# A third pair of seven-product units in three of the four blocks of keys and values

## The chip, the cores and the metric

One NeuronCore of a Trainium2 chip runs the whole kernel. The metric is the device time of one execution in microseconds (us). The engines are named as in the profile: PE (TensorE, the products), PEld (its loading of the stationary operand), DVE (VectorE), ACT (ScalarE), POOL (GpSimd) and SP (SyncE, which issues the transfers).

## The reference

One layer of an encoder on 256 frames of width 2048 in float32: a half-step feed-forward (SwiGLU), a mixer, a cross-attention to 256 memory tokens, and a second half-step feed-forward. The change touches the cross-attention only, and there the projection of the memory to keys and values:

```python
def mem_cross_attention(h, mem_h, w_q, w_kv, w_o):
    b, s, _ = h.shape
    q = (h @ w_q).reshape(b, s, XATTN_HEADS, XATTN_HEAD_DIM)
    kv = (mem_h @ w_kv).reshape(b, mem_h.shape[1], 2, XATTN_HEADS, XATTN_HEAD_DIM)
    k, v = kv[:, :, 0], kv[:, :, 1]
    logits = jnp.einsum('bshd,bmhd->bhsm', q, k).astype(jnp.float32) * (XATTN_HEAD_DIM ** -0.5)
    p = jax.nn.softmax(logits, axis=-1).astype(v.dtype)
    o = jnp.einsum('bhsm,bmhd->bshd', p, v).reshape(b, s, D_MODEL)
    return o @ w_o
```

There are 4 heads of 512 columns; `w_kv` is 2048 x 4096, keys in the first half of the columns, values in the second.

## The kernel before

**Precision by parts.** Every float32 operand of a product is held as a high part (rounded to the type fp32r) and a low part (what the rounding left). A product of two such operands takes three matmuls: high by high, high by low, low by high (`products`, L357 to L362). In this text a *product* is one such matmul of 128 x 128 by 128 x 512.

**Units.** All weights pass through the kernel once, in units of 1 MB (128 x 2048 float32). A unit is loaded by SP into one of three `raw` tiles, split by ACT (high part `wh`, L1579) and DVE (low part `wl`, L453; near the end of a block POOL takes 768 of the 2048 columns), and used by PE. The class `Stream` writes all this out in order: splits run two units ahead of PE (`AHEAD`), the load of unit u + 3 is issued behind the split of unit u, and `st.op(f, n)` puts other work behind n further units. `wh` and `wl` have three buffers each. A scheduler then settles the order in each engine's queue by a timeline of its own.

**Blocks.** A block is eight units: all 2048 rows of a weight matrix, 256 rows a unit, by 1024 columns. A plain unit (`unit_p` in `block_s`) does 24 products. The cross-attention has blocks of queries, then, for each half of the heads, a block of keys and a block of values, then blocks of the output projection. In the loop over b near the end of the change's region, each block of keys is followed by the turning of the keys (`turn_K`), the logits and softmax of two heads (`logits`, then `probs`, which turns the probabilities with PE transposes at L1341), all placed among the first units of the block of values; the products of values with probabilities (`values`, L1358) fall among the first units of the block after.

**Seven products.** Some units are computed as a 2 x 2 product with seven multiplications in the place of eight (`seven`, L493 to L509, Strassen's scheme in Winograd's form): 21 products instead of 24. For this the unit's weights need sums (`split_seven`: DVE makes T in three operations at L486; ACT and DVE split T into `wh` and `wl`, 4 x 512 columns, and three of the four raw quarters into `xh` and `xl`, L279 and L280), and the pair of row groups of the activations needs sums too, made once for all blocks that use that pair (`Sums.make`, L424 to L437, kept in the tile `ye` and partly in `xs` itself). The results P1 to P7 go to two pairs of PSUM accumulators: P2, P4, P3 and P0 hold what plain units add to as well, P1, P6 and P7, P5 only serve the turned units. `combine` (L574 to L579) and `join` (L589) bring them together at the end of the block.

**PSUM.** One pool of four tiles serves accumulators, transposes, logits and the products with values alike. The pair for P1, P6, P7, P5 can thus only be opened when the softmax or `values` has given its tiles back.

**Homes.** In the cross-attention the tiles for T, `xh` and `xl` are not their own: `shared_tile` takes them in turn from a list of tags (`homes`). For keys and values, T lies in `sg` (two buffers of 2048 columns, which also hold the blocks' combined results) and `xh` and `xl` in `att` (two buffers of 1536 columns). So the raw parts of one unit fill both buffers of `att`. Keys and values themselves lie in `kv`, two buffers of 2048 columns.

**Order.** `kv_sums` names the pairs with sums, here 0 and 4. `KV_ORDER` is the order of the eight units in each block, so units 0 and 4 stand at the fourth and seventh places.

Of the kernel before, what the change touches and what calls it, by code (L numbers as in the profile page):

```python
# [15 lines left out]
D = 2048  # L16
# [4 lines left out]
NB = 512  # L21
# [78 lines left out]
def build(ctx, tc, I, out):  # L100
# [89 lines left out]
    xs = main.tile([P, KT, 2, S], F32R, tag="xs", name="xs")  # L190
# [79 lines left out]
    def among_weights(f):  # L270


        scalar, vector = behind_weights(f)
        latest["vector"] = vector
        if scalar is not None:
            latest["scalar"] = scalar
# [349 lines left out]
    def wload(dst, w, k0, n, n0, cols=NB):  # L626
        nc.sync.dma_start(
            dst, w[k0 * P : (k0 + n) * P, n0 : n0 + cols].rearrange("(k p) n -> p k n", p=P)
        )
# [9 lines left out]
    def wwide(w, n0, k0=0, nk=KT):  # L639

        def src(k):
            def load(raw):
                raw = raw.rearrange("p (k n) -> p k n", n=2 * NB)
                if len(loaded) < 3:
                    for kk in range(2):
                        parts = (0, NB) if not loaded else (0,)
                        for c in parts:
                            n = 2 * NB // len(parts)
                            wload(raw[:, kk : kk + 1, c : c + n], w, k + kk, 1, n0 + c, n)
                else:  # L650
                    wload(raw, w, k, 2, n0, 2 * NB)
                next(first_loads, None)
                loaded.append(1)
            return load
        return [src(k0 + k) for k in range(0, nk, 2)]
# [557 lines left out]
    for b in range(2):  # L1213
        block_b(wblock(w_in, (4 + b) * NB), xs, ev_v(b))
        for i in range(2):
# [12 lines left out]
                 "xl": [("att", 3 * NB, 2), ("PT", D, 1)]}  # L1228
    Q_HOMES = {"T": [("sg", D, 2)], "xh": [("att", 3 * NB, 2)],
               "xl": [("PT", D, 1), ("att", 3 * NB, 2)]}  # L1230
    KV_HOMES = {"T": [("sg", D, 2)], "xh": [("att", 3 * NB, 2)], "xl": [("att", 3 * NB, 2)]}

    def homes(of):
        return lambda: scope.update(shared={tag: list(of[tag]) for tag in of})
# [27 lines left out]
    def mem_fold(c):  # L1262

        v = four(ptile(uid("tm")))
        for j in range(4):
            for h in range(2):
                nc.tensor.transpose(  # L1267
                    v[:, j, h * P : (h + 1) * P],
                    xa[f"mem{h}"][:, c * NB + j * P : c * NB + (j + 1) * P], ident,
                )  # L1270
        split_four(xs, 4 * c, v, G_MEM)
# [10 lines left out]
    w_q, w_kv, w_o = I["xattn_w_q"][0], I["xattn_w_kv"][0], I["xattn_w_o"][0]  # L1282
# [2 lines left out]
    q_sums, Q_ORDER = Sums("ye", xs, (4, 5), True, 2), ((0, 1, 2, 3, 6, 4, 5, 7),  # L1285
                                                        (0, 1, 4, 2, 5, 3, 6, 7))
    Q_SEVENS = ((4,), (4, 5))
    kv_sums, KV_ORDER = Sums("ye", xs, (0, 4), True, 2), (1, 5, 2, 0, 3, 6, 4, 7)
    held = {}

    def ev_Q(b):
# [10 lines left out]
    def turn_K(h):  # L1302
        v = rows_turned(held["K", h])
        K = xa["K", h] = xt("K", [P, 4, 2, M], F32R, tag="kv", bufs=2)
        split(K[:, :, 0, :], K[:, :, 1, :], v)

    def ev_V(b):
        def evict(j, c):
            V = xa["V", 2 * b + j] = xt("V", [P, 2, 2, XHD], F32R, tag="kv", bufs=2)
            split(V[:, :, 0, :], V[:, :, 1, :], c)  # L1310
        return evict

    def logits(h):
        ps = ptile(uid("pl"))
        for t in range(2):
            tok = slice(t * P, (t + 1) * P)
            parts = [(d, a, b) for d in range(4) for a, b in ((0, 0), (0, 1), (1, 0))]
            for i, (d, a, b) in enumerate(parts):
                nc.tensor.matmul(  # L1319
                    ps[:, t, :M], ys[:, 4 * h + d, a, tok], xa["K", h][:, d, b, :],  # L1320
                    start=i == 0, stop=i == 11,
                )
        scale = XHD ** -0.5
        nm, sm = xt("nm", [P, 2], bufs=2), xt("sm", [P, 2], bufs=2)
        nc.vector.tensor_reduce(out=nm, in_=ps[:, :, :M], axis=AX.X, op=ALU.max)
        nc.vector.tensor_scalar_mul(nm, nm, -scale)
        pr = xa["P", h] = xt("P", [P, 2, M], bufs=2)
        for t in range(2):
            nc.scalar.activation(
                pr[:, t, :], ps[:, t, :M], AF.Exp, scale=scale, bias=nm[:, t : t + 1],  # L1330
                accum_out=sm[:, t : t + 1],
            )
        nc.vector.reciprocal(out=sm, in_=sm)
        for t in range(2):
            nc.vector.tensor_scalar_mul(pr[:, t, :], pr[:, t, :], sm[:, t : t + 1])

    def probs(h):
        ps = ptile(uid("pt"))
        for mtile in range(2):
            for t in range(2):  # L1340
                nc.tensor.transpose(  # L1341
                    ps[:, mtile, t * P : (t + 1) * P], xa["P", h][:, t, mtile * P : (mtile + 1) * P], ident
                )
        if h % 2 == 0:
            xt("PT", [P, D], F32R)
        PT = xa["PT", h] = xa["PT"][:, h % 2 * 4 * S : (h % 2 + 1) * 4 * S].rearrange(
            "p (m a s) -> p m a s", m=2, a=2
        )
        split(PT[:, :, 0, :], PT[:, :, 1, :], ps[:, :, :S])

    def values(h):
        for p in range(2):
            ps = ptile(uid("pv"))
            for d in range(2):
                col = slice((2 * p + d) * P, (2 * p + d + 1) * P)
                parts = [(m, a, b) for m in range(2) for a, b in ((0, 0), (0, 1), (1, 0))]
                for i, (m, a, b) in enumerate(parts):
                    nc.tensor.matmul(  # L1358
                        ps[:, d, :S], xa["V", h][:, m, a, col], xa["PT", h][:, m, b, :],
                        start=i == 0, stop=i == 5,  # L1360
                    )
            split_pair(ys, 4 * h + 2 * p, ps[:, :, :S])
# [3 lines left out]
    for b in range(2):  # L1366
# [3 lines left out]
        if b == 0:  # L1370
            for c, after in enumerate((5, 7, 6, 9)):
                st.op(lambda c=c: mem_fold(c), after)
    st.op(homes(KV_HOMES))
    for g, after in zip(kv_sums.pairs, (0, 2)):
        st.op(lambda g=g: among_weights(lambda: kv_sums.make(g)), after)
    for b in range(2):
        block_s(wwide(w_kv, b * 2 * NB), xs, kv_sums, KV_ORDER, lambda j, c, b=b: held.__setitem__(
            ("K", 2 * b + j), c))
        for j in (1, 0):
            h = 2 * b + j  # L1380
            st.op(lambda h=h: turn_K(h), 1)
        for h in (2 * b, 2 * b + 1):
            st.op(lambda h=h: logits(h), 2)
            st.op(lambda h=h: probs(h), 3)
        block_s(wwide(w_kv, D + b * 2 * NB), xs, kv_sums, KV_ORDER, ev_V(b))
        for h in (2 * b, 2 * b + 1):
            st.op(lambda h=h: values(h), 1)
# [211 lines left out]
def program(shapes):  # L1599
    import concourse.bacc as _bacc  # L1600

    nc = _bacc.Bacc("TRN2", target_bir_lowering=False, num_devices=1)
    args = {
        name: nc.dram_tensor(f"in_{name}", shapes[name], F32, kind="ExternalInput").ap()
        for name in _INS
    }
    out = nc.dram_tensor("out", _OUT, F32, kind="ExternalOutput").ap()
    with tile.TileContext(nc, schedule_with_timeline_sim=True) as tc, ExitStack() as ctx:
        build(ctx, tc, args, out)
    return nc  # L1610
# [10 lines left out]
```

## Time and profile before

| | |
|---|---|
| median of 3 runs | 2083.8 us (2082.58 to 2084.51) |
| the profiled execution: its own time | 2082.87 us |
| its span, first to last instruction | 2081.1 us |
| granted clock of PE, mean | 0.999 |

Rows of the timeline give the start in us, the length in us, the engine, line, operation, out<-in, and in brackets the idle time before it and what ended it. Rows of grouped views end with busy us, mean ns of one, idle us before. Rows of windows give the stretch, its length, then busy us (and count) of PE, PEld, DVE, ACT and POOL, then the granted clock, the share of the DMA engines, and GB/s. In the timeline a product's row lasts longer than the distance to the next one's start, since products overlap; the ends of products are modelled.

### The profile page before, as it was taken

The numbers are of one execution on the slowest core, as the hardware profiler recorded it, in microseconds if no ns is written. First come the engines' busy times: TensorE is split into PE (matmuls) and PEld (weight loads), VectorE is DVE, ScalarE is ACT, GpSimd is POOL, SyncE is SP. The second block draws the span as 40 slices with busy tenths as digits, with TensorE's granted clock in tenths as the row PEclk, the third lists the DMA queues.
The fourth block names the chain that finished last, engine by engine and source line by source line (L and its number), as shares of the span: only waits on it lengthen the run. The fifth ranks groups of instructions, "written<-read, shape, count | busy, mean of one in ns | idle before, by whom it ended". The sixth has DMA issues, their size and how long they took to land.

```text
span 2081.1 us, 24343 instructions
## 1 busy us (share of the span) xinstructions
PE 2069.6 (99%) x9660; PEld 1727.6 (83%) x9660; DVE 1786.6 (86%) x1670; ACT 1138.7 (55%) x1128; POOL 98.4 (5%) x87
## 2 busy tenths in 40 slices
PE   9999999999999999999999999999999999999998
PEld 7888888888888888888888888888888888888886
DVE  7998899989998677679788777879988999889987
ACT  7655455644654545455755444656554555545554
POOL 0000000000000000000000000000100010000001
PEclk9999999999999999999999999999999999999999
DMA  7666666566656755557655455666576665676664
GB/s 264 207 201 227 235 223 219 185 223 239 227 199 218 249 167 182 162 185 272 226 179 190 162 182 180 205 222 203 181 242 212 237 207 193 223 242 222 210 226 151
DMA packets 131178, 435.95 MB, mean 209 GB/s; under 512 B 9844, under 2 KB 13528, under 8 KB 130680
## 3 DMA queue, kind: packets, MB, share of 16 engines
q1 hardware_dynamic: 130888, 433.86, 61.9%
q8 instruction: 76, 1.25, 0.2%
q10 hardware_dynamic: 176, 0.53, 0.1%
q14 instruction: 38, 0.31, 0.0%
HBM read 417.58 MB, written 16.78 MB: 209 GB/s over the span
## 4 chain that ended last, share of the span: by engine, by line
PE 99%; DMA 0%; DVE 0%; ACT 0%; SPq 0%; DVEq 0%; issue 0%; ACTq 0%
PE pt L362 59%; PE pt L507 27%; PE pa L347 7%; PE pb L362 2%; PE ph L780 1%; PE pl L1319 1%; PE pv L1358 1%; PE px L791 1%; PE pp L1012 0%; PE pe L362 0%; DMA x<-in_x 0%; PE pa L1039 0%; PE po L1161 0%; PE tm L1267 0%; PE px L717 0%; PE pq L1148 0%
## 5 line engine op out<-in xcount | busy, mean ns | idle before, releaser
L362 PE MATMUL pt<-wh,xs 128*128 128x512 f32 x2128 | 682.4, 390 | 0.1
L453 DVE TENSOR_TENSOR wl<-raw,wh 128x2048 fp32r<-128x2048 f32 (+1 forms) x256 | 552.1, 2162 | 141.7 <-ACT wh L1579 141.3
L1579 ACT CAST wh<-raw 128x2048 fp32r<-128x2048 f32 x256 | 489.4, 1913 | 300.7 <-PE pt L362 134.5
L362 PEld LDWEIGHTS pt<-wh,xs 128*128 128x128 f32 x2128 | 398.7, 188 | 81.9 <-ACT xs L236 0.4
L362 PE MATMUL pt<-wh,ys 128*128 128x512 f32 x1472 | 463.9, 389 | 0.0
L489 ACT CAST wh<-T 128x1024 fp32r<-128x1024 f32 x236 | 248.1, 1055 | 366.7 <-DVE T L486 355.8
L362 PE MATMUL pt<-wl,xs 128*128 128x512 f32 x1064 | 414.5, 390 | 0.0
L362 PEld LDWEIGHTS pt<-wh,ys 128*128 128x128 f32 x1472 | 276.2, 188 | 56.9
L362 PE MATMUL pt<-wl,ys 128*128 128x512 f32 x736 | 286.8, 390 | 0.0
L453 DVE TENSOR_TENSOR wl<-T,wh 128x2048 fp32r<-128x2048 f32 (+1 forms) x118 | 264.7, 2243 | 0.8 <-ACT wh L489 0.4
L362 PEld LDWEIGHTS pt<-wl,xs 128*128 128x128 f32 x1064 | 199.8, 188 | 41.0
L280 DVE TENSOR_TENSOR xl<-raw,xh 128x1536 fp32r<-128x1536 f32 x118 | 206.7, 1751 | 18.9 <-ACT xh L279 18.9
L279 ACT CAST xh<-raw 128x1536 fp32r<-128x1536 f32 x118 | 174.6, 1480 | 44.0 <-PE pt L507 35.1
L486 DVE TENSOR_TENSOR T<-T,raw 128x512 f32<-128x512 f32 x236 | 162.9, 690 | 6.2
L362 PEld LDWEIGHTS pt<-wl,ys 128*128 128x128 f32 x736 | 138.2, 188 | 28.6
L486 DVE TENSOR_TENSOR T<-raw 128x1024 f32<-128x1024 f32 x118 | 143.8, 1218 | 0.5
L507 PE MATMUL pt<-wh,xs 128*128 128x512 f32 x364 | 141.8, 390 | 0.0
L457 POOL TENSOR_TENSOR wl<-raw,wh 128x768 fp32r<-128x768 f32 x40 | 74.1, 1852 | 1376.2 <-DVE wl L453 1339.2
L507 PE MATMUL pt<-xh,xs 128*128 128x512 f32 x364 | 135.8, 389 | 0.0
L347 PE MATMUL pa<-xs,wh 128*128 128x512 f32 x384 | 135.6, 397 | 0.0
L507 PE MATMUL pt<-wh,xe 128*128 128x512 f32 x320 | 124.3, 389 | 0.0
L347 PE MATMUL pa<-xs,wl 128*128 128x256 f32 x384 | 106.8, 282 | 0.0
(248 smaller groups left out, 2312.4 us busy)
## 6 DMA issues: line engine op xcount, KB each, us to landing
raw<-in_ffn_w_down SPq DMA_DIRECT2D x88, 1024.0 KB, 5.6
raw<-in_ffn_w_up SPq DMA_DIRECT2D x80, 1024.0 KB, 5.0
raw<-in_ffn_w_gate SPq DMA_DIRECT2D x77, 1024.0 KB, 5.1
raw<-in_w_in SPq DMA_DIRECT2D x32, 1024.0 KB, 5.3
raw<-in_xattn_w_kv SPq DMA_DIRECT2D x32, 1024.0 KB, 5.0
raw<-in_w_out SPq DMA_DIRECT2D x16, 1024.0 KB, 5.6
raw<-in_xattn_w_q SPq DMA_DIRECT2D x16, 1024.0 KB, 5.6
raw<-in_xattn_w_o SPq DMA_DIRECT2D x16, 1024.0 KB, 5.6
```

What stands on the lines that cost most here:

```text
L279: in_turn("scalar", lambda: nc.scalar.copy(hi, src))
L280: in_turn("vector", lambda: nc.vector.tensor_tensor(out=lo, in0=src, in1=f32(hi), op=ALU.subtract))
L347: nc.tensor.matmul(o, w, x, start=k == 0 and i == 0, stop=last and i == 1)
L362: nc.tensor.matmul(ps, a, w, start=first and i == 0, stop=last and i == 2)
L453: in_turn("vector", lambda: nc.vector.tensor_tensor(out=lo[:, :n], in0=src[:, :n], in1=f32(hi[:, :n]), op=ALU.subtract))
L457: rest = nc.gpsimd.tensor_tensor(out=lo[:, n:], in0=src[:, n:], in1=f32(hi[:, n:]), op=ALU.subtract)
L486: in_turn("vector", lambda: nc.vector.tensor_tensor(out=o, in0=a, in1=b, op=ALU.add))
L489: in_turn("scalar", lambda: nc.scalar.copy(th[:, c], t[:, c]))
L507: nc.tensor.matmul(banks[n], x, w, start=n in fresh and j == 0, stop=n in ends and j == 2)
L780: nc.tensor.transpose(v[:, i, h * P : (h + 1) * P], g[:, h, i * P : (i + 1) * P], ident)
L791: nc.tensor.transpose(v[:, j, h * P : (h + 1) * P], x[:, h, j * P : (j + 1) * P], ident)
L1579: in_turn("scalar", lambda: nc.scalar.copy(hi, raw))
```

## The change

A third pair, 2, joins the sums of keys and values, and its unit is computed with seven products in three of the four blocks: both blocks of values and the second block of keys. The first block of keys keeps its order and its two seven-product units, since there the sums of pair 2 are only being made. In the three other blocks the order changes so that the turned units stand at places 4 (pair 0), 6 (pair 4) and 7 (pair 2). The list of homes for `xh` and `xl` is written out by turns: the middle one of the three takes its raw parts to the tiles of keys and values (`kv`), the two others to `att` as before.

```diff
-    KV_HOMES = {"T": [("sg", D, 2)], "xh": [("att", 3 * NB, 2)], "xl": [("att", 3 * NB, 2)]}
+    KV_TURNS = [("att", 3 * NB, 2)] * 2 + [("att", 3 * NB, 2), ("kv", D, 2), ("att", 3 * NB, 2)] * 3
+    KV_HOMES = {"T": [("sg", D, 2)], "xh": KV_TURNS, "xl": KV_TURNS}
...
-    kv_sums, KV_ORDER = Sums("ye", xs, (0, 4), True, 2), (1, 5, 2, 0, 3, 6, 4, 7)
+    kv_sums = Sums("ye", xs, (0, 4, 2), True, 3)
+    KEY_ORDER, KV_ORDER = (1, 5, 2, 0, 3, 6, 4, 7), (1, 5, 3, 0, 6, 4, 2, 7)
...
-    for g, after in zip(kv_sums.pairs, (0, 2)):
+    for g, after in zip(kv_sums.pairs, (0, 2, 5)):
         st.op(lambda g=g: among_weights(lambda: kv_sums.make(g)), after)
     for b in range(2):
-        block_s(wwide(w_kv, b * 2 * NB), xs, kv_sums, KV_ORDER, lambda j, c, b=b: held.__setitem__(
-            ("K", 2 * b + j), c))
+        block_s(wwide(w_kv, b * 2 * NB), xs, kv_sums, KV_ORDER if b else KEY_ORDER,
+                lambda j, c, b=b: held.__setitem__(("K", 2 * b + j), c),
+                sevens=() if b else (0, 4))
```

## The prediction

> **What bounds the kernel now.** I read the page first (busy shares, the chain of waits), then the waits of PE, then the windows of the cross-attention, then its timeline.
>
> ```profile
> span 2081.1 us, 24343 instructions
> PE 2069.6 (99%) x9660; PEld 1727.6 (83%) x9660; DVE 1786.6 (86%) x1670; ACT 1138.7 (55%) x1128; POOL 98.4 (5%) x87
> PE 99%; DMA 0%; DVE 0%; ACT 0%; SPq 0%; DVEq 0%; issue 0%; ACTq 0%
> ```
>
> ```profile
> PE pwarm L206 <- POOL ident masks.py:199: 1.4, 1, 1.4
> PE px L717 <- DMA x<-in_x: 0.8, 1, 0.8
> ```
>
> The chain is PE from end to end, and the view of waits puts only two against it, both at the start. A product left out is therefore time saved, and a wait of PE is time added. Nothing later makes it good, as PE has no slack to give back.
>
> ```profile
> 1135.00:1186.00 51.00, 51.00 (x261) 43.36 (x261) 36.47 (x36) 25.00 (x27) 3.47 (x3) 1.00 0.49 165
> 1186.00:1234.00 48.00, 48.00 (x236) 40.68 (x235) 34.31 (x28) 22.91 (x20) 3.74 (x3) 1.00 0.53 175
> 1234.00:1284.00 50.00, 50.00 (x257) 42.57 (x256) 35.66 (x35) 23.38 (x25) 3.02 (x3) 1.00 0.51 167
> 300.00:420.00 120.00, 120.00 (x539) 99.55 (x538) 114.70 (x88) 71.03 (x59) 7.42 (x4) 1.00 0.61 201
> ```
>
> The first three windows are the three blocks that change (first values, second keys, second values); the fourth is a stretch of the first feed-forward. The columns after the times are busy us of PE, PEld, DVE, ACT, POOL. DVE is 72% busy in the three blocks and 96% in the feed-forward, whose PE is as dense. So on average DVE has room for more work here; what decides is the order inside a block.
>
> The one place late in the run where PE does wait is too short for the view of waits, but the timeline has it, in the block of queries:
>
> ```profile
> 1062.74 0.39 PE L507 MATMUL pt<-xl,xs 128*128 128x512 f32 x1
> 1062.97 0.39 PE L507 MATMUL pt<-xh,xs 128*128 128x512 f32 x1
> ...
> 1066.49 0.50 PE L507 MATMUL pt<-xl,xs 128*128 128x512 f32 x1
> 1066.83 0.39 PE L507 MATMUL pt<-xh,xs 128*128 128x512 f32 x1
> ...
> 1068.98 0.50 PE L507 MATMUL pt<-wl,xs 128*128 128x512 f32 x1
> ```
>
> ```profile
> 1063.17 1.48 ACT L279 CAST xh<-raw 128x1536 fp32r<-128x1536 f32 x1 [11.12 <-PE pt L507]
> 1064.55 1.99 ACT L489 CAST wh<-T 128x1024 fp32r<-128x1024 f32 x2
> ```
>
> ```profile
> 1064.68 1.76 DVE L280 TENSOR_TENSOR xl<-raw,xh 128x1536 fp32r<-128x1536 f32 x1 [4.33 <-ACT xh L279]
> 1066.63 2.29 DVE L453 TENSOR_TENSOR wl<-T,wh 128x2048 fp32r<-128x2048 f32 x1 [0.19 <-ACT wh L489]
> ```
>
> These rows give four prices. A product costs 0.227 us from start to start (1062.74 to 1062.97), though each row lasts 0.39. When PE has read the last of a 7-product unit's raw low part at time a, the next such unit's raw parts may be cast into the freed tile: ACT starts at a + 0.43, the new low raw part reaches PE at a + 3.75 (1066.49), the low part of the sums at a + 6.24 (1068.98). The first product after a wait comes 0.34 later instead of 0.227, so each wait costs 0.11 more than itself.
>
> **The change part by part.** *Products removed.* A plain unit has 24 products, a 7-product one 21. One more unit is turned in each of three blocks: 9 products by 0.227 = -2.04 us. That is all it can win, 0.10% of the time.
>
> *The third set of sums* adds seven VectorE and two ScalarE operations, once, in the first block of keys. The order of the built program puts them between the two splits that end and begin here:
>
> ```profile
> L424 DVE TENSOR_TENSOR j<-xs 128x512 f32<-128x512 f32 x1 | 0.7, 686 | 0.0
> L286 DVE TENSOR_TENSOR ye<-j,ye 128x384 fp32r<-128x384 f32 x1 | 0.6, 550 | 0.0
> L432 DVE TENSOR_TENSOR j<-j 128x128 f32<-128x128 f32 x1 | 0.3, 293 | 0.0
> ```
>
> ```profile
> 1121.67 2.29 DVE L453 TENSOR_TENSOR wl<-raw,wh 128x2048 fp32r<-128x2048 f32 x1
> 1126.80 1.49 DVE L453 TENSOR_TENSOR wl<-raw,wh 128x1280 fp32r<-128x1280 f32 x1 [2.85 <-ACT wh L1579]
> ```
>
> ```profile
> 1129.37 0.39 PE L362 MATMUL pt<-wh,xs 128*128 128x512 f32 x1
> ```
>
> Six of them, 0.69 + 5 x 0.29 = 2.1 us, go ahead of the first row, and 2.85 us stand idle behind it; the seventh (0.55) comes after the second row, where DVE waits again: nothing. The unit of the first row is then split by 1126.1, 3 us before PE begins it (third row); without the gap that would be the cover.
>
> *More split work.* Each turned unit adds three sums and a raw low part on DVE, 1.22 + 2 x 0.69 + 1.76 = 4.4 us, against about 14 us that DVE idles in each block:
>
> ```profile
> L1579 ACT CAST wh<-raw 128x2048 fp32r<-128x2048 f32 x7 | 13.4, 1913 | 10.5 <-PE pt L362 6.8 <-issue 3.4 <-ACT wh L1579 0.3
> L453 DVE TENSOR_TENSOR wl<-raw,wh 128x2048 fp32r<-128x2048 f32 x4 | 9.2, 2290 | 3.4 <-ACT wh L1579 3.4
> ...
> L280 DVE TENSOR_TENSOR xl<-raw,xh 128x1536 fp32r<-128x1536 f32 x2 | 3.5, 1756 | 4.2 <-ACT xh L279 4.2
> ...
> L486 DVE TENSOR_TENSOR T<-T,raw 128x512 f32<-128x512 f32 x4 | 2.8, 690 | 0.1
> L486 DVE TENSOR_TENSOR T<-raw 128x1024 f32<-128x1024 f32 x2 | 2.4, 1218 | 0.0
> ```
>
> Weight transfers keep their number and order; the loads behind places 6 and 7 start up to 2 us later and are wanted over 5 us after that. Cost nothing.
>
> *Middle unit's raw parts in the tiles of keys and values.* In a block of values the cast of the middle unit's high raw part now stands in ACT's queue ahead of the first softmax, and waits until PE has done the first head's logits:
>
> ```profile
> 1153.53 0.69 DVE L1325 TENSOR_REDUCE nm<-pl 128x2 f32<-128x512 f32 x1 [1.56 <-PE pl L1319]
> 1156.86 0.17 DVE L1333 RECIPROCAL sm<-sm 128x2 f32<-128x2 f32 x1 [2.43 <-ACT P L1329]
> 1157.06 0.62 DVE L1335 TENSOR_SCALAR P<-P,sm 128x256 f32<-128x256 f32 x2
> ```
>
> ```profile
> 1154.51 1.28 ACT L1329 ACT_TABLE_LOAD   x1 [4.86 <-DVE nm L1326]
> ```
>
> Logits end at 1153.5, the cast runs to 1155.0, so the table load starts 0.5 us late. Following both queues on with the durations above, the first head's probabilities are ready at 1158.8 and the second's at 1166.5.
>
> ```profile
> 1158.73 0.39 PE L507 MATMUL pt<-xh,xs 128*128 128x512 f32 x1
> ...
> 1160.55 0.60 PE L1341 MATMUL pt<-ident,P 128*128 128x128 f32 x4
> ...
> 1161.22 0.40 PE L362 MATMUL pt<-wh,xs 128*128 128x512 f32 x1
> ```
>
> PE begins place 4 at 1158.73; four transposes cost 1161.22 - 1160.55 - 0.227 = 0.44. In the new order PE turns the first probabilities after 13 products (1161.7, 2.9 us to spare) and the second after 20 + 9 more (1168.7, 2.2 us to spare). Nothing, by those margins. In the second block of keys they wait for the first values' last product; 27 products, 6.1 us, lie between that and their use, and the low part takes 1.76: nothing.
>
> *Places 6 and 7 side by side.* The raw parts of place 7 go into the tile of place 4. Both before and after, these are free late, as PE puts off the twelve of place 4's products that go into P1, P6, P7 and P5 until the softmax gives up its PSUM tiles. Before, a plain unit still lay between:
>
> ```profile
> 1169.67 0.39 PE L507 MATMUL pt<-xl,xs 128*128 128x512 f32 x1
> ...
> 1176.24 0.39 PE L507 MATMUL pt<-xl,xs 128*128 128x512 f32 x1
> ```
>
> ```profile
> 1170.09 1.48 ACT L279 CAST xh<-raw 128x1536 fp32r<-128x1536 f32 x1 [5.79 <-PE pt L507]
> ```
>
> From the last read to the next use 6.57 us passed, and 3.75 are needed. In the new order 13 products and three transposes lie between, 14 x 0.227 + 0.33 = 3.50. So in each block of values, counted from a:
> - wait 1, low raw part: ready 3.75, reached 3.50: 0.25.
> - wait 2, low part of the sums: eight products on PE reaches it at 3.75 + 0.34 + 7 x 0.227 = 5.68; ready 6.24: 0.56.
> - wait 3: all 18 products of P7 and P5 of the three units now come in a row, from 7.26 on, because their accumulator is only freed by the second head's probabilities. The sixth, at 8.39, is the last to read place 4's weights, and only then may ACT cast place 8: 8.39 + 0.43 + 1.91 + 0.04 + 2.29 + 0.06 = 13.12. PE does the other twelve and two of place 8 and stands before its low part at 11.79: 1.33.
>
> Sum 2.14, with 3 x 0.11 behind the waits 2.47, and 0.09 for transposes that now stand in three groups instead of two: 2.56 a block, 5.1 us for both. Behind the waiting product everything on PE stands; ACT and DVE only gain lead. The bounds of the unseen wait 3 are nothing (place 8 finds another buffer) and, if the cast had to wait for all 18, 4.0; I take 1.33, as the built program names the sixth. In the second block of keys no probabilities hold the accumulators: 29 products lie between place 4's last raw read and place 7's first, 6.8 us. No wait.
>
> *Sum.* -2.04 + 5.1 = +3.1 us. The profiled run took 2082.87 (span 2081.1 and 1.8 around it): 2086.0. The median of the runs is 0.93 above it: **2086.9**.
>
> **The rivals.**
> - *The waits don't come* and the nine products are won: 2083.8 - 2.0 = 2081.8. For it: 2.47 us a block rests on margins of 0.25 to 1.33, and DVE is 72% busy. Against: the queries' block shows two of the three waits at just these distances.
> - *The softmax takes over* (slower). ACT casts the middle unit's parts between the two exponentials, DVE sums between the two heads, and PE waits in order for the second head's transposes. It decides once the chain is more than the 2.2 us late. If a raw low part and a low part of sums (1.76 + 2.29) came ahead of the second probabilities, 1.85 us a block would be added: 2086.9 + 3.7 = 2090.6. Against: the built order has them behind.
> - *PE's clock falls in the waits* (slower). If the 24 products of place 8 ran at half rate after a wait, 5.4 us a block would be added: 2097.8. The granted clock is the column before the DMA share; it is 1.00 in the windows above and lower only where PE did nothing for microseconds, after its last product:
>
> ```profile
> 2076.00:2081.00 5.00, 0.00 (x0) 0.00 (x0) 0.49 (x2) 0.20 (x1) 0.00 (x0) 0.59 0.63 236
> ```
>
> The Trainium skill ("TensorE: Matmul & The Clock Gate", "HAM oscillation — how this bites in real kernels") puts the limit at PE gaps over about 3.4 us; by that rule waits of 1.33 leave the sum as it is, and no run here shows the limit itself.
>
> **How the numbers follow.** The forecast 0.60, no waits 0.20, softmax 0.16, clock 0.04. A measurement of this kernel can tell about 0.2%, 4.2 us, from no change. The forecast's own range is 2085.3 to 2088.5 (0.8 us a block either way); about an eighth of it lies beyond 2088.0. Slower by over 0.2%: 0.08 + 0.15 + 0.04 = 0.27. Faster by as much needs more than the nine products: 0.01. Within: 0.72. The range takes in the no-wait case and the softmax's up to its price, and leaves out the clock: 2081.3 to 2090.5.
>
> **What would show it.** In the profile after: nine L362 and L507 products fewer; three gaps between starts of products in each block of values, before a low raw part, a low part of sums from T, and the low part of the plain unit that ends the block, the last the longest; DVE at about 80% there; no gap before the transposes of P and none in the second block of keys. Wrong: no gaps (rival one), gaps before the transposes of P (rival two), products 0.4 us apart or a clock under 1 (rival three).

## The result, and the profile after

| | before | after |
|---|---|---|
| median | 2083.39 us (2082.58 to 2084.51) | 2086.61 us (2085.95 to 2089.36) |
| span of the profiled execution | 2081.1 us | 2084.1 us |

The ratio is 1.0016, with a 95% interval of 1.001 to 1.0022: slower by 3.2 us, where 3.1 were forecast (2086.9, reckoned from a median before of 2083.8). Below are the line of busy times after, and the windows of the three blocks that changed (first values, second keys, second values; the columns are those of the prediction). Each window ends at the product at which the window of before ends.

```profile
PE 2069.3 (99%) x9651; PEld 1724.8 (83%) x9651; DVE 1800.0 (86%) x1689; ACT 1143.4 (55%) x1136; POOL 98.6 (5%) x87
```

```profile
1135.05:1187.85 52.80, 51.30 (x258) 42.51 (x258) 38.90 (x39) 26.44 (x29) 2.42 (x3) 1.00 0.44 144
1187.85:1235.15 47.30, 47.30 (x233) 40.10 (x232) 39.41 (x33) 24.57 (x22) 5.00 (x3) 1.00 0.56 195
1235.15:1286.98 51.83, 50.31 (x254) 41.74 (x253) 38.06 (x38) 24.53 (x27) 2.37 (x2) 1.00 0.50 165
```

Nine matmuls are gone (9660 to 9651). PE is busy for all of the second block of keys, but leaves 1.5 us open in each block of values, where no window before showed any. The three blocks together grew by 2.9 us (149.0 to 151.9). The timeline of PE in the first block of values (start, length, then what runs) says where:

```profile
1168.80 0.27 PE L1343 MATMUL pt<-ident,P 128*128 128x128 f32 x1
...
1169.14 0.40 PE L507 MATMUL pt<-xl,xs 128*128 128x512 f32 x1
...
1170.74 0.49 PE L1343 MATMUL pt<-ident,P 128*128 128x128 f32 x3
...
1172.46 0.39 PE L507 MATMUL pt<-xh,ye 128*128 128x512 f32 x1
1172.90 0.50 PE L507 MATMUL pt<-xl,xs 128*128 128x512 f32 x1
1173.24 0.40 PE L507 MATMUL pt<-xh,xs 128*128 128x512 f32 x1
...
1174.64 0.40 PE L507 MATMUL pt<-wh,xs 128*128 128x512 f32 x1
1175.33 0.50 PE L507 MATMUL pt<-wl,ye 128*128 128x512 f32 x1 [0.30 <-DVE wl L453]
...
1177.54 0.40 PE L507 MATMUL pt<-wh,ye 128*128 128x512 f32 x1
...
1180.49 0.61 PE L362 MATMUL pt<-wh,xs 128*128 128x512 f32 x2
1182.26 0.50 PE L362 MATMUL pt<-wl,xs 128*128 128x512 f32 x1 [1.15 <-DVE wl L453]
```

A wait is what the distance of two starts has over 0.227. From 1172.46 to 1172.90 that is 0.21, ahead of place 7's low raw part; from 1174.64 to 1175.33 it is 0.47, ahead of the low part of its sums; and between the second product of place 8 (1180.49 + 0.23 = 1180.72) and its first with a low part (1182.26) it is 1.31. The start behind a wait comes 0.34 later (1172.90 to 1173.24): a refill of 0.11 each. The brackets tell less than that, 0.30 and 1.15, and nothing at the first wait, as the modelled end of a product hides part of a gap: waits this short are read from starts. The chain behind them, from ScalarE's and VectorE's timelines:

```profile
1169.57 1.48 ACT L279 CAST xh<-raw 128x1536 fp32r<-128x1536 f32 x1 [6.62 <-PE pt L507]
...
1172.85 0.58 ACT L285 CAST PT<-pt 128x512 fp32r<-128x512 f32 x1
1177.97 3.71 ACT L1582 CAST wh<-raw 128x2048 fp32r<-128x2048 f32 x2 [4.54 <-PE pt L507]
```

```profile
1165.62 0.61 DVE L1337 TENSOR_SCALAR P<-P,sm 128x256 f32<-128x256 f32 x2
...
1171.09 1.76 DVE L280 TENSOR_TENSOR xl<-raw,xh 128x1536 fp32r<-128x1536 f32 x1 [4.25 <-ACT xh L279]
1172.99 2.29 DVE L453 TENSOR_TENSOR wl<-T,wh 128x2048 fp32r<-128x2048 f32 x1
1175.20 0.68 DVE L286 TENSOR_TENSOR PT<-pt,PT 128x512 fp32r<-128x512 f32 x1
1179.91 3.69 DVE L453 TENSOR_TENSOR wl<-raw,wh 128x2048 fp32r<-128x2048 f32 x2 [4.03 <-ACT wh L1582]
```

ScalarE stands idle for 6.62 us until PE has read place 4's raw low part (1169.14 + 0.43 = 1169.57), VectorE for 4.25 us until that cast is done. The rows with PT are the split of the second head's turned probabilities, which gives back the PSUM tile for P7 and P5. PE had begun the last three transposes at 1170.74, but in both queues this split stands behind place 7's, so the tile is free only at 1175.20 + 0.68 = 1175.88. Later ScalarE waits again for the sixth product of P7 and P5 (1177.54 + 0.43 = 1177.97) and VectorE for ScalarE. Neither engine is short of time on the whole where PE waits for it: each has waited for PE first.

### The profile page after: what moved, and what is told of

Its sections match the earlier page's. It is cut to its first block, busy times and chain, and to the rows that moved or that the text cites. A ratio compares the mean times of both kernels' runs of the same rounds, so it can differ in the third digit from the quotient of the medians.

```text
span 2084.1 us, 24353 instructions
## 1 busy us (share of the span) xinstructions
PE 2069.3 (99%) x9651; PEld 1724.8 (83%) x9651; DVE 1800.0 (86%) x1689; ACT 1143.4 (55%) x1136; POOL 98.6 (5%) x87
## 3 DMA queue, kind: packets, MB, share of 16 engines
q8 instruction: 76, 1.25, 0.2%
## 4 chain that ended last, share of the span: by engine, by line
PE 98%; DVE 1%; ACT 0%; issue 0%; DMA 0%; SPq 0%; DVEq 0%; ACTq 0%
PE pt L362 58%; PE pt L507 27%; PE pa L347 6%; PE pb L362 2%; PE ph L780 1%; DVE wl L453 1%; PE pl L1321 1%; PE pv L1360 1%; PE px L791 1%; PE pp L1012 0%; PE pe L362 0%; DMA x<-in_x 0%; ACT wh L1582 0%; ACT wh L489 0%; PE pa L1039 0%
## 5 line engine op out<-in xcount | busy, mean ns | idle before, releaser
L362 PE MATMUL pt<-wh,xs 128*128 128x512 f32 x2080 | 666.6, 390 | 0.6 <-ACT xs L236 0.6
L453 DVE TENSOR_TENSOR wl<-raw,wh 128x2048 fp32r<-128x2048 f32 (+1 forms) x253 | 545.2, 2161 | 138.4 <-ACT wh L1582 138.0
L1582 ACT CAST wh<-raw 128x2048 fp32r<-128x2048 f32 x253 | 483.4, 1913 | 301.5 <-PE pt L362 126.7
L489 ACT CAST wh<-T 128x1024 fp32r<-128x1024 f32 x242 | 254.1, 1054 | 373.9 <-DVE T L486 361.6
L362 PEld LDWEIGHTS pt<-wh,xs 128*128 128x128 f32 x2080 | 389.8, 188 | 80.8 <-ACT xs L236 0.9
L362 PE MATMUL pt<-wl,xs 128*128 128x512 f32 x1040 | 405.4, 391 | 2.3 <-DVE wl L453 2.3
L453 DVE TENSOR_TENSOR wl<-T,wh 128x2048 fp32r<-128x2048 f32 (+1 forms) x121 | 271.6, 2245 | 2.9 <-ACT wh L489 2.6
L362 PEld LDWEIGHTS pt<-wl,xs 128*128 128x128 f32 x1040 | 195.3, 188 | 43.0 <-DVE wl L453 3.1
L280 DVE TENSOR_TENSOR xl<-raw,xh 128x1536 fp32r<-128x1536 f32 x121 | 211.9, 1752 | 13.7 <-ACT xh L279 13.5
L507 PE MATMUL pt<-wh,xs 128*128 128x512 f32 x376 | 145.8, 389 | 0.0
L507 PE MATMUL pt<-xh,xs 128*128 128x512 f32 x376 | 140.8, 390 | 0.0
```

The costliest lines, as they stand in the source:

```text
L280: in_turn("vector", lambda: nc.vector.tensor_tensor(out=lo, in0=src, in1=f32(hi), op=ALU.subtract))
L362: nc.tensor.matmul(ps, a, w, start=first and i == 0, stop=last and i == 2)
L453: in_turn("vector", lambda: nc.vector.tensor_tensor(out=lo[:, :n], in0=src[:, :n], in1=f32(hi[:, :n]), op=ALU.subtract))
L489: in_turn("scalar", lambda: nc.scalar.copy(th[:, c], t[:, c]))
L507: nc.tensor.matmul(banks[n], x, w, start=n in fresh and j == 0, stop=n in ends and j == 2)
L1582: in_turn("scalar", lambda: nc.scalar.copy(hi, raw))
```

## The experiments

The theory is that of the prediction: place 4's twelve products for P1, P6, P7 and P5 are put off until the softmax gives up its PSUM tiles, so the tiles of its raw parts and weights are let go late, and places 7 and 8 are split late. The rows above add why the second head's tile comes so late: its split stands behind place 7's own in the queues of ScalarE and VectorE. The rival that the windows leave open is load: VectorE has more to do with each third unit. A third question is what a wait does to PE's clock. Each kernel is compared with runs of the kernel before made together with it; those had medians of 2082.9 to 2083.2 us.

| kernel | median, us | ratio to before, 95% interval | waits left, without refills (us) |
|---|---|---|---|
| k1_only | 2082.53 | 0.9998 (0.9989 to 1.0007) | none |
| last_high_first | 2083.88 | 1.0004 (0.9995 to 1.0012) | values: 0.21, 0.49 |
| turned_before | 2080.83 | 0.999 (0.9982 to 0.9999) | none |
| sevens_567 | 2083.35 | 1.0001 (0.9992 to 1.001) | values: 0.98 |
| raws_in_att | 2089.37 | 1.003 (1.0018 to 1.0041) | values and second keys: 0.35, 0.48, 1.17 |
| probs_first | 2082.82 | 0.9999 (0.999 to 1.0008) | values: 0.64 |
| order_only | 2085.30 | 1.0009 (1.0 to 1.0018) | values: 0.75, 0.28 |
| first_keys_too | 2082.28 | 0.9995 (0.9986 to 1.0004) | first keys: 0.35, 0.60, 0.17 |
| casts_3 | 2098.01 | 1.0072 (1.0055 to 1.0089) | values: 0.21, 0.48, 3.3, then a slow clock |
| casts_6 | 2110.22 | 1.0131 (1.0116 to 1.0146) | values: 0.21, 0.47, 9.1, then a slow clock |

Most of the intervals reach 1. What tells these kernels apart is the waits in their timelines, which came out the same to some hundredths of a us in both blocks of values; the medians agree with them.

**The third unit without the waits: k1_only.**

```diff
-        block_s(wwide(w_kv, D + b * 2 * NB), xs, kv_sums, KV_ORDER, ev_V(b))
+        block_s(wwide(w_kv, D + b * 2 * NB), xs, kv_sums, KEY_ORDER, ev_V(b), sevens=(0, 4))
...
-    KV_TURNS = [("att", 3 * NB, 2)] * 2 + [("att", 3 * NB, 2), ("kv", D, 2), ("att", 3 * NB, 2)] * 3
+    KV_TURNS = [("att", 3 * NB, 2)] * 4 + [("att", 3 * NB, 2), ("kv", D, 2), ("att", 3 * NB, 2)] + [("att", 3 * NB, 2)] * 2
```

> The third pair is turned in the second block of keys alone; both blocks of values are as before the change. Theory (the loss sits in the three waits of each block of values): 3 products fewer than before, no wait: 2083.4 - 3 x 0.227 = 2082.7 us, no gap over 0.33 us between starts of products from the first keys to the last values. Rival (the extra sums and split work load VectorE too much wherever a third unit is turned): waits in the second block of keys too, where VectorE is the busiest, and a time at or above 2083.4.

The plain unit 2 of the values multiplies here by activations that the sums of pair 2 have overwritten, which changes no count and no size; the kernel's result is not that of the layer, and it serves for timing alone. Measured: 2082.53, no wait. The windows of this kernel for the second keys and second values:

```profile
1185.95:1233.27 47.32, 47.32 (x233) 40.12 (x232) 38.47 (x32) 24.41 (x22) 3.95 (x3) 1.00 0.54 177
1233.27:1283.28 50.01, 50.01 (x257) 42.57 (x256) 35.61 (x35) 23.38 (x25) 2.78 (x3) 1.00 0.52 168
```

VectorE takes on 38.47 - 34.31 = 4.2 us in the block of keys (4.4 were reckoned for a turned unit) and PE never stops. A third unit as such costs PE nothing.

**Taking away the third wait alone: last_high_first.** In place 8 of the values, the 16 products with the high part of the weights go first.

```diff
...
+                if g in high_first:
+                    for low in (False, True):
+                        for j in (1, 0):
+                            for h in range(2):
+                                for kk in range(2):
+                                    half(held["banks"][names[j, h]], act, 2 * g + kk, h, wh[:, kk, j],
+                                         wl[:, kk, j], low, g == order[-1] and kk == 1 and low)
+                    return
...
```

> The changed kernel, with the plain unit at place 8 of the blocks of values doing its 16 products with the high part of the weights first and the 8 with the low part behind them. Theory: the third wait goes, since 12 products cover the cast of the high part and 28 (6.4 us) its low part, which is ready 4.7 us after the freeing product; waits 1 and 2 stay (0.21 and 0.47): 2086.6 - 2 x (1.31 + 0.11) = 2083.8 us. Rival (VectorE is simply behind in these blocks): the wait comes back at the next unit, in the block after: 2086.6.

```profile
1181.01 3.79 PE L368 MATMUL pt<-wh,xs 128*128 128x512 f32 x16
1184.64 1.98 PE L368 MATMUL pt<-wl,xs 128*128 128x512 f32 x8
1186.45 0.39 PE L362 MATMUL pt<-wh,xs 128*128 128x512 f32 x1
```

PE's timeline runs through place 8 without a gap and into the next block, while waits 1 and 2 stand as they were. 2083.88 against 2083.8 expected: the third wait went and didn't come back.

**Taking away all three by order: turned_before.** Place 6's products stand behind the second head's transposes (`ahead`), place 7's raw casts behind the split of these probabilities (`behind`).

```diff
+        if behind:
+            latest["scalar"], latest["vector"] = behind.pop()
         split_weights(rh, rl, raw[:, NB:])
...
+                if g in ahead:
+                    with tc.issue_after(ahead.pop(g).ins):
+                        seven(held["banks"], act, sums, g, fresh, ends, weights, order)
+                    return
...
+        if h % 2:
+            ahead[4] = last
+        turned[h] = split(PT[:, :, 0, :], PT[:, :, 1, :], ps[:, :, :S])
...
+        st.op(lambda b=b: behind.append(turned[2 * b + 1]), 4)
```

> The changed kernel, with two orders set in the blocks of values: place 6's products on PE stand behind the transposes of the second head's probabilities, and the casts of place 7's raw parts behind the split of these probabilities. Nothing else is changed, VectorE and ScalarE do the same work. Theory (the waits come from place 4's twelve products being put off until the second head gives back its PSUM tile): 15 products lie between those transposes and P7/P5, the 12 products of P7 and P5 stand ahead of place 7, no wait is left: 2083.4 - 2.0 + 0.1 = 2081.5 us. Rival (VectorE's load): the same work and so the same 2.3 us of waits a block, 2086.6. Second rival: PE now waits for the second head's probabilities ahead of the transposes, some 1 us a block, 2083.5.

PE's timeline in the first values, the split of the second head's probabilities on ScalarE and on VectorE, and this kernel's window of that block:

```profile
1167.98 0.49 PE L1351 MATMUL pt<-ident,P 128*128 128x128 f32 x3
...
1175.14 0.39 PE L511 MATMUL pt<-wh,xs 128*128 128x512 f32 x1
1175.37 0.39 PE L511 MATMUL pt<-xl,xs 128*128 128x512 f32 x1
```

```profile
1168.51 0.58 ACT L285 CAST PT<-pt 128x512 fp32r<-128x512 f32 x1 [5.82 <-PE pt L1351]
```

```profile
1169.13 0.69 DVE L286 TENSOR_TENSOR PT<-pt,PT 128x512 fp32r<-128x512 f32 x1 [2.56 <-ACT PT L285]
```

```profile
1134.80:1185.13 50.33, 50.33 (x258) 42.73 (x257) 40.30 (x40) 26.56 (x29) 3.68 (x3) 1.00 0.50 167
```

Counted from the start of the two windows, the last three transposes start 2.5 us earlier than in the changed kernel (there at 1170.74, here at 1167.98), and their split follows at once on ScalarE and is done on VectorE at 1169.82 instead of 1175.88. P7 and P5 follow without a wait, and place 7's low raw part is reached at its turn, 0.23 behind its neighbour. VectorE is busier in this block than in the changed kernel's (40.30 in 50.3 us against 38.90 in 52.8) and PE waits for nothing: load isn't the cause. At 2080.83 us this version is ahead of both kernels, by 2.2 us of the kernel before.

**Half of that order: probs_first.** Only `behind`, not `ahead`.

> Like turned_before, but only the casts of place 7's raw parts are put behind the split of the second head's probabilities; PE's transposes of these stay where the change has them, one ahead and three inside place 4's P1 and P6. Theory: the three waits go, and one new one comes ahead of P7, since four products lie between the third transposes and P7 and the two splits take 1.9 us from there: 0.6 + 0.11 a block, 2082.3 to 2083.4 us. Rival (it is enough that the splits come early): no wait, 2080.9.

```profile
1170.80 0.49 PE L1347 MATMUL pt<-ident,P 128*128 128x128 f32 x3
...
1171.83 0.39 PE L511 MATMUL pt<-wh,ye 128*128 128x512 f32 x1
1172.69 0.50 PE L511 MATMUL pt<-wh,xs 128*128 128x512 f32 x1 [0.48 <-DVE PT L286]
```

The three waits are gone, and PE waits 0.64 for the accumulator itself, 1.9 us behind the last transposes, as expected. Only the order of the casts was changed here, so it is the split of the second head's probabilities, and with it the release of that PSUM tile, that the three waits hang on. PE's own order (`ahead`) takes away the 0.64 that is left.

**Another order of places: sevens_567.**

```diff
-        block_s(wwide(w_kv, D + b * 2 * NB), xs, kv_sums, KV_ORDER, ev_V(b))
+        block_s(wwide(w_kv, D + b * 2 * NB), xs, kv_sums, (1, 5, 3, 6, 0, 4, 2, 7), ev_V(b))
```

> The changed kernel with the 7-product units of the blocks of values at places 5, 6 and 7 (order 1, 5, 3, 6, 0, 4, 2, 7). Theory: place 5 is held up less than place 4 was, 26 products lie between its last raw read and place 7's low part, so the three waits go; one new wait of about 0.75 us comes ahead of P1, as PE has only 5 instructions between the first head's transposes and the accumulators that these free: 2083.4 - 2.0 + 2 x 0.86 = 2083.1 us. Rival (VectorE's load): three units in a row, each 6.6 us of VectorE against 4.8 us of PE, make it worse than the change: over 2087.

```profile
1168.52 0.60 PE L1343 MATMUL pt<-ident,P 128*128 128x128 f32 x4
1168.87 0.48 PE L507 MATMUL pt<-wh,xs 128*128 128x512 f32 x1
1169.19 0.60 PE L1343 MATMUL pt<-ident,P 128*128 128x128 f32 x4
1170.52 0.50 PE L507 MATMUL pt<-xh,xs 128*128 128x512 f32 x1 [0.73 <-DVE PT L286]
```

Three turned units in a row, and one wait: PE stands ahead of P1 until the first head's probabilities are split. A product follows the start of four transposes after 0.35 when nothing holds it up (1168.52 to 1168.87); here it comes at 1170.52 instead of 1169.54, a wait of 0.98 where 0.75 was expected. The time is 2083.35 against 2083.1. The load rival said over 2087.

**The order with two turned units: order_only.**

```diff
-        block_s(wwide(w_kv, D + b * 2 * NB), xs, kv_sums, KV_ORDER, ev_V(b))
+        block_s(wwide(w_kv, D + b * 2 * NB), xs, kv_sums, KV_ORDER, ev_V(b), sevens=(0, 4))
```

The list of homes is changed as well, so that the turned unit at place 6 keeps its raw parts in the tiles of keys and values.

> The new order of the blocks of values with two 7-product units, at places 4 and 6; place 7 is plain there (it multiplies activations that the sums of pair 2 have overwritten, which changes no count and no size). Products as in k1_only. Theory (the order itself costs, as place 4's weights are still let go late): the low part of place 8 is ready 3.9 us behind the sixth product of P7 and P5, and reached after 13 products, 2.95: a wait of 1.0, then 0.2 for the columns that GpSimd subtracts: 1.4 with refills a block, 2083.2 - 0.7 + 2.8 = 2085.3 us. Rival (only the third unit makes the waits): 2082.5 us, as k1_only.

The time is 2085.30, with waits of 0.75 and 0.28 at place 8 instead of 1.0 and 0.2: with refills 1.25 a block instead of 1.4, so the time fits better than its terms. It has the products of k1_only and takes 2.6 us more, each set against its own runs of the kernel before (+2.1 and -0.5). The order of places costs by itself, without the third unit in these blocks.

**One part undone: raws_in_att.** The middle unit's raw parts share `att` with the two others.

```diff
-    KV_TURNS = [("att", 3 * NB, 2)] * 2 + [("att", 3 * NB, 2), ("kv", D, 2), ("att", 3 * NB, 2)] * 3
+    KV_TURNS = [("att", 3 * NB, 2)]
```

> The changed kernel with one part undone: the middle 7-product unit's raw parts go to the tiles of place 4 and 7 (att), not to those of keys and values. Theory (counted from place 4's last raw read a, which now stands right behind place 5): place 6's low raw part is ready at a + 3.75 and reached at a + 3.4, its low part of sums 0.56 late as in the block of queries, place 7's low parts and place 8's 0.1 to 0.2 late each; the second head's probabilities come earlier, since ScalarE and VectorE no longer put place 6's parts in between, so P7 and P5 are not put off. Together about 1.2 of waits and 0.45 of refills a block against 2.3: 2084.2 to 2085.2 us, the longest wait under 0.7 and the 1.3 us wait at place 8 gone. Rival (the tiles of keys and values are what makes the close order bearable): each of places 6 and 7 waits for the one before, over 4 us a block, 2090 or more.

This expectation failed: 2089.37. PE and VectorE in the first values:

```profile
1177.49 0.39 PE L507 MATMUL pt<-wh,xs 128*128 128x512 f32 x1
1178.89 0.50 PE L507 MATMUL pt<-xl,xs 128*128 128x512 f32 x1 [1.01 <-DVE xl L280]
```

```profile
1172.30 2.29 DVE L453 TENSOR_TENSOR wl<-T,wh 128x2048 fp32r<-128x2048 f32 x1
1174.50 1.22 DVE L486 TENSOR_TENSOR T<-raw 128x1024 f32<-128x1024 f32 x1
1175.76 1.42 DVE L486 TENSOR_TENSOR T<-T,raw 128x512 f32<-128x512 f32 x2
1177.09 1.75 DVE L280 TENSOR_TENSOR xl<-raw,xh 128x1536 fp32r<-128x1536 f32 x1
```

Two things were left out of it. VectorE makes its splits in order, so place 7's sums T, 2.6 us, which wait for nothing themselves, stand behind place 6's late ones; that makes place 7's raw part 1.17 late instead of 0.2. And the close order of places holds in the second block of keys too, where the same three waits came. A fourth wait of only 0.03 brings a refill too. Together that is about 2.5 us in each of three blocks against 2.3 in each of two: 7.4 - 4.7 = 2.7 us more than the changed kernel, and 2.8 were measured. So the tiles of keys and values are a part of the change that pays, and they are why its block of keys has no wait.

**The first block of keys as well: first_keys_too.** turned_before, with the third unit in all four blocks.

```diff
...
-        block_s(wwide(w_kv, b * 2 * NB), xs, kv_sums, KV_ORDER if b else KEY_ORDER,
-                lambda j, c, b=b: held.__setitem__(("K", 2 * b + j), c),
-                sevens=() if b else (0, 4))
+        block_s(wwide(w_kv, b * 2 * NB), xs, kv_sums, KV_ORDER,
+                lambda j, c, b=b: held.__setitem__(("K", 2 * b + j), c),
+                sevens=None)
```

> turned_before with the third pair turned in the first block of keys too, in the same order of places. Theory: nothing holds the accumulators there, so three products fewer and no wait: 2080.8 - 0.7 = 2080.1 us. Rival (VectorE also makes the sums in that block): a wait before place 7's low part, 2081 or more.

```profile
1126.06 0.50 PE L511 MATMUL pt<-wh,xs 128*128 128x512 f32 x1 [0.19 <-ACT xs L285]
...
1127.46 0.50 PE L511 MATMUL pt<-xh,ye 128*128 128x512 f32 x1 [0.44 <-ACT ye L285]
```

The rival held: the sums of pair 2 are just being made there, and PE waits for them (xs, ye), 1.1 us and three refills against 0.7 won. The time is 2082.28, 1.4 behind turned_before; the waits explain 0.8 of this.

**What a longer wait does to the clock: casts_3 and casts_6.** Place 8's cast is done three and six times, so that the third wait grows.

```diff
...
-                in_turn("scalar", lambda: nc.scalar.copy(hi, raw))
+                for _ in range(3 if u in cast_again else 1):
+                    in_turn("scalar", lambda: nc.scalar.copy(hi, raw))
```

> The changed kernel, with place 8's cast of the high part done three times over in the blocks of values (the same values each time), to lengthen the third wait. From the sixth product of P7 and P5: casts done at 0.43 + 3 x 1.91 = 6.2, PE comes there at 2.7, so a wait of 3.4 us ahead of the first product of place 8, then 1.7 ahead of the first with the low part. If the clock stays at 1.00 after such waits: each block 3.9 us more, 2086.6 + 7.7 = 2094.3 us, products 0.227 apart at once behind the wait. If PE's clock falls (the third rival of the prediction): products further apart behind the waits and a granted clock under 1 in those microseconds, up to 5.4 us more a block, 2105.

> The same with six casts: done at 0.43 + 6 x 1.91 = 11.9, a wait of 9.2 us, then 1.7. With the clock unmoved: 9.6 more a block than the changed kernel, 2086.6 + 19.2 = 2105.8 us. With a clock that falls in the wait: products further apart behind it, and a time above that by what the slow stretch costs, up to 5.4 us a block, 2116.6.

The waits came as expected, 3.3 and 9.1 us, and after both the clock was at half. PE's timeline and windows of casts_3 in the first values (the granted clock is the column before the DMA share), then windows of casts_6 in both blocks of values:

```profile
1180.74 0.39 PE L508 MATMUL pt<-wh,ye 128*128 128x512 f32 x1
1184.27 1.22 PE L362 MATMUL pt<-wh,xs 128*128 128x512 f32 x2 [3.14 <-ACT wh L1586]
...
1188.05 0.63 PE L362 MATMUL pt<-wl,xs 128*128 128x512 f32 x1
1188.47 1.05 PE L362 MATMUL pt<-wh,xs 128*128 128x512 f32 x2
```

```profile
1183.00:1183.50 0.50, 0.00 (x0) 0.00 (x0) 0.00 (x0) 0.50 (x1) 0.00 (x0) 0.95 0.00 0
1183.50:1184.00 0.50, 0.00 (x0) 0.00 (x0) 0.00 (x0) 0.50 (x1) 0.00 (x0) 0.50 0.00 0
...
1190.00:1190.50 0.50, 0.50 (x3) 0.36 (x3) 0.50 (x1) 0.00 (x0) 0.00 (x0) 0.72 1.01 418
```

```profile
1186.00:1187.00 1.00, 0.00 (x0) 0.00 (x0) 0.00 (x0) 0.97 (x2) 0.00 (x0) 0.70 0.00 0
...
1196.50:1197.00 0.50, 0.50 (x4) 0.42 (x3) 0.50 (x1) 0.00 (x0) 0.00 (x0) 0.86 1.10 230
...
1295.00:1296.00 1.00, 0.00 (x0) 0.00 (x0) 0.00 (x0) 0.97 (x2) 0.00 (x0) 0.81 0.00 0
...
1309.00:1309.50 0.50, 0.50 (x3) 0.38 (x2) 0.50 (x2) 0.00 (x0) 0.17 (x1) 0.72 0.94 180
```

At half clock products start 0.427 us apart. Over the sums with an unmoved clock the two kernels took 2098.0 - 2094.3 = 3.7 and 2110.2 - 2105.8 = 4.4 us more, 1.9 and 2.2 a block.

## Why the prediction was right

- *Nine products*: shown. 9 fewer matmuls, and turned_before, in which no wait is left, is 2.2 us below the kernel before, where 2.04 were reckoned.
- *Three waits in each block of values, none in the second keys*: shown, by the place, the cause and the size. Counted from a = 1169.14, the read of place 4's raw low part: low raw part ready at 3.76 (3.75 forecast), wait 0.21 (0.25); low part of the sums at 6.19 (6.24), wait 0.47 (0.56); sixth product of P7 and P5 at 8.40 (8.39), place 8's low part at 13.12 (13.12), wait 1.31 (1.33). The queries' block of the kernel before had given the chain link by link, and the built program the number of products in between.
- *The sum*: right, and its closeness to a tenth is partly luck. The terms as measured give 2 x 2.33 - 2.04 = 2.6 us, and the three blocks grew by 2.9, where 3.1 were reckoned. Some 0.35 us of the 3.2 lie outside the span: the profiled time is 2086.24 - 2084.1 = 2.14 above its span after and 2082.87 - 2081.1 = 1.77 before, where the prediction took 1.8 for both. No run shows why.
- *Cost of a block*: 1.99 of waits and 0.34 of refills, 2.33 against 2.47. The refills were right; waits 1 and 2 came 0.04 and 0.09 short: PE reached both points 0.05 later than reckoned (3.55 and 5.73 behind a), and the low part of the sums was ready 0.05 sooner.
- *The bounds of wait 3* (nothing to 4.0): the value in between was the right one because ScalarE is released by one product, the sixth, which the timeline shows 0.43 us ahead of the cast.
- *Sums, split work, tiles of keys and values at no cost*: shown by k1_only, with no wait in the blocks of keys or in the values that follow, and for the blocks of values by turned_before.
- *Rival one, no waits*: refuted here, and true of turned_before, so it was a matter of the order in the queues and not of the third unit. The prediction had the late release of the tile, and its time, right; that it is late because place 7's splits stand ahead of the probabilities' shows in the queues, and probs_first, which moves only these splits, is rid of all three waits.
- *Rival two, softmax*: refuted. The second head's probabilities are ready at 1165.62 + 0.61 = 1166.23 and taken at 1168.80, a margin of 2.6 us where 2.2 were reckoned.
- *Rival three, clock*: refuted for waits of 1.31; the windows of the blocks stay at 1.00. Waits of 3.3 us do bring it (the last section has what was seen in between), and its price was too high: 1.9 to 2.2 us a block, not 5.4, as the clock is back before the 24 products are done.

Two side remarks of the prediction failed, without weight for the sum. VectorE was to be about 80% busy in the blocks of values; it was 74% (38.90 of 52.80), as the waits lengthen the block and over 1 us of its work slid into the next one, and is 80% (40.30 of 50.33) in turned_before. And "ACT and DVE only gain lead" behind a waiting product is wrong here for VectorE: it stands idle for ScalarE and PE first, and its last split in the block starts 1.7 us ahead of the window's end (1186.18 to 1187.85) where it started 2.7 ahead before (1183.28 to 1186.00).

## What to carry to other kernels

Where the tensor engine never waits, cost a change by counting: for each tile that it shares, the products between the last read of the old contents and the first use of the new, against the chain of cast and subtraction in between; a neighbouring stretch of the same kernel often shows that chain's length. When a wait turns up behind an engine that is not busy, follow what that engine itself waited for: here the way back was to turn one head's probabilities 2.5 us earlier and to split them ahead of the next unit's casts, with no work taken away from VectorE or ScalarE.

## What was not expected of the hardware

The clock moved on a grid. From the windows above, where a window's mean between 1.00 and 0.50 gives the instant of the step, it fell at 1183.45 and was back at 1190.28 in casts_3 (6.83 us), and at 1186.40 and 1196.64 (10.24), and 1295.62 and 1309.28 (13.66) in casts_6: two, three and four times 3.41 us. The two falls of casts_6 lie 109.22 us apart, 32 times 3.41, so the grid runs on through products and waits. In casts_3 the clock fell 2.3 us after PE's last product had ended (1180.74 + 0.39 = 1181.13, a modelled end). In the first block of casts_6 it fell 5.3 us after it (1180.75 + 0.39 = 1181.14): there the grid point before the fall, 1186.40 - 3.41 = 1182.99, came 1.85 us into the wait, and the clock stayed. So 2.3 us without products ahead of a grid point were enough and 1.85 were not; that the idle time ahead of a point is what decides is inferred from these places, not shown by itself. A wait shorter than a grid step can thus halve the clock, and the same wait can cost differently in two places: behind the last wait of each block of casts_6 products ran at half clock for 4.25 us in the first block (1192.39 to 1196.64) and for 5.48 in the second (1303.80 to 1309.28). The Trainium skill ("TensorE: Matmul & The Clock Gate", "Part 1: The HAM clock gate (the "warmup" mystery)") has a free-running window of 3413 ns, which the multiples agree with; the limit of about 3.4 us on gaps, cited in the prediction from the same page, is too wide by these runs, and the measurement decides.
